# ScalarE's cast of the next pair ahead of VectorE's work on the present one, and four pairs in sevens in blocks 1 to 9 of a decoder layer's gate-and-up products

## The chip, the cores and the metric

The kernel runs on one core of a Trainium2 chip. Its engines are TensorE (PE in the profile: matmuls; PEld: its weight loads), VectorE (DVE), ScalarE (ACT), GpSimd (POOL) and SyncE (SP, which here issues the DMA transfers). The metric is the device time of one execution in microseconds; less is better.

## The reference

The reference is one decoder layer on 256 tokens of width 2048, in float32: a half-FFN, a pair of token mixers (retention and sliding-window attention), a second half-FFN, and a gated embedding, with a layer norm after each. What the change touches most are the two half-FFNs (width 5632):

```
def swiglu(x, w_gu, w_down):
    g, u = jnp.split(x @ w_gu, 2, axis=-1)
    return (jax.nn.silu(g) * u) @ w_down
...
h = layer_norm(alpha * h + 0.5 * swiglu(h, w_ffn1_gu[i], w_ffn1_down[i]), ln_g[i, 0], ln_b[i, 0])
...
mixed = (jax.nn.sigmoid(gate_r) * ret_branch + jax.nn.sigmoid(gate_a) * att_branch) @ w_mix_out[i]
...
h = layer_norm(alpha * h + 0.5 * swiglu(h, w_ffn2_gu[i], w_ffn2_down[i]), ln_g[i, 2], ln_b[i, 2])
ple = jax.nn.sigmoid(h @ w_ple_gate[i]) * (p[i] @ w_ple_proj[i])
```

## The kernel before

**Products in two parts.** Each float32 operand is split into a high part in the format fp32r (`hi`, a cast by ScalarE) and the rest (`lo`, the operand minus `hi`, a subtraction by VectorE). A product is then three matmuls, lo by hi, hi by hi and hi by lo (`Sum.add`, L341 to L343).

**Blocks, pairs and sevens.** A product with a large weight is made in blocks of 1024 columns. A block is a list of units; a unit is a pair of tiles along the inner dimension, and a block over the width of 2048 has eight. A unit of class `Unit` (a plain pair, kind "P") loads one weight tile `raw` of 128x2048, has ScalarE cast it to `hi` (L101) and VectorE subtract `lo` (L102), and takes TensorE 8 products, or 24 matmuls. A unit of class `Seven` (kind "S") makes the same 2 by 2 block product from 7 products, 21 matmuls, in Strassen's way; for that the weights must first be added up:

| step | engine and line | tile |
|---|---|---|
| cast of three quarters of the raw tile | ScalarE, L191 | hb |
| sums u (2 quarters, then 1 and 1) | VectorE, L192, L196, L197 | u |
| casts of the sums (twice 1024) | ScalarE, L193, L198 | hu |
| subtraction lb | VectorE, L202 | lb |
| subtraction lu | VectorE, L205 | lu |

These names carry a prefix of the weight: `lf_gu` in the profile is lo of a plain pair of `f1_gu` or `f2_gu`, `luf_gu` is lu of a seven. The first plain pairs of a block come first and the last pair is plain, so that the end of the sevens (`fold`, `seven_common`, L416) lies inside the block: ScalarE copies a first sum out of PSUM into a tile `eve` (L420), and VectorE makes three operations on it (L423 to L425), which free two of the four PSUM tiles of two banks each. The next block starts in these. VectorE then adds the two other PSUM tiles (L743, twice), ScalarE applies SiLU (L745), and VectorE multiplies gate and up (L748). The result is transposed by TensorE after the second unit of the next block (`turned`, L699, tiles f1t and f2t), and ScalarE copies the transposes out (L700).

**Gate and up.** `w_gu` of each half-FFN is 11 blocks, j = 0 to 10, in the order of `gu_units`. Block 0 is plain. The other odd blocks have four sevens, the even ones three.

**A planner writes the order.** All instructions are in an order fixed by the program. The units of the whole kernel stand in one list, `plan`; `load` issues their DMA on SyncE's queue, up to three units ahead; `step` makes the next unit, a few VectorE instructions at a time; and `pump` takes steps until an estimated VectorE time reaches an estimated TensorE time (`clock`). All of these tiles come from one pool of 23 slots (`SLOTS`). `room` counts what is used of a limit that `weights(n)` sets for each stage: a unit takes 1 slot for its load, 2 (plain) or 5 (seven) while it is made, and keeps 2 or 4 until its matmuls are done. In the gate-and-up blocks the limit falls from 17 to 11 as the activations fill the pool:

```
weights(SLOTS - 5 - (j + 1) // 2 - (2 if j == KF // 4 - 1 else 0))
```

Each engine works through its queue in order. An instruction that waits, for a transfer, another engine or a free slot, holds up all that stands behind it on the same engine.

**The mixers' last product and the norms.** `MIXERS` names the sevens of the mixers' blocks; `w_mix` has two blocks. The last three units of the second (`HELD`) are multiplied first for one half of the tokens, then for the other, so that the norm of the first half runs beside the second. `EVENTS` places the parts of each norm between these units and the first units of the next product: "s" scales a group of columns for one half of the tokens, "t" turns it (transposes, ScalarE's cast, VectorE's subtraction into `ht`). The third entry is the norm ahead of the embedding (`w_pg`).

Of the kernel before, what the change touches and what calls it, by code (L numbers as in the profile page):

```python
# [9 lines left out]
F32R = mybir.dt.float32r  # L10
I32 = mybir.dt.int32
AF = mybir.ActivationFunctionType
ALU = mybir.AluOpType
PSUM = bass.MemoryType.PSUM

P = 128
# [10 lines left out]
KF = FF // P  # L27
# [7 lines left out]
MATMUL = 0.227  # L35
# [18 lines left out]
    ("w_ret", 0): ("PPSPSPSP", (0, 1, 2)),  # L54
    ("w_ret", 1): ("PPSPSPSP", (0, 1, 2)),
    ("w_mix", 0): ("PPPPSPSP", (4, 5)),
    ("w_mix", 1): ("PSPSPPPP", (4, 5)),
}

BIG = 3.0e38  # L60
# [12 lines left out]
        "a6": "c0 m0 s00", "b6": "t00 c1 m1 s10", "c5": "t10", "c6": "s01", "d1": "s11", "d4": "t01", "d5": "t11",  # L73
    },
    {
        "a6": "c0 m0 s00 s01", "b4": "t00", "b6": "t01 c1 m1 s10 s11", "c4": "s02", "c6": "t10", "c7": "t11",
        "d1": "s12", "d4": "t02", "d7": "t12",
    },
)
# [3 lines left out]
def layer(ctx: ExitStack, tc: tile.TileContext, io):  # L83
    nc = tc.nc
    sync, act, dve, pe = nc.sync, nc.scalar, nc.vector, nc.tensor
# [3 lines left out]
    slots = ctx.enter_context(tc.tile_pool(name="slots", bufs=SLOTS))  # L89
# [7 lines left out]
    def slot(shape, dt, name):  # L97
        return slots.tile(shape, dt, tag="slot", name=name)

    def split(dst_hi, dst_lo, src):  # L100
        act.copy(dst_hi, src)  # L101
        dve.tensor_tensor(dst_lo, src, dst_hi, ALU.subtract)  # L102


    plan = []
    GROUP_AT = {"rg": 8, "gr": 21, "ga": 29}

    def halves_of(key):

        name, b, p = key  # L110
        if name.endswith("_gu"):
            return [io[name][2 * b : 2 * b + 2, 1 - c, p // 2, :, p % 2 * 2 : p % 2 * 2 + 2, :] for c in range(2)], True
        if name in GROUP_AT or name in ("w_ret", "w_att"):
            w, at = (io["w_in_f"], GROUP_AT[name]) if name in GROUP_AT else (io[name], 0)
            at += 4 * b
            return [w[at + 2 * c : at + 2 * c + 2, p // 2, :, p % 2 * 2 : p % 2 * 2 + 2, :] for c in range(2)], True
        return [io[name][2 * b + c, p] for c in range(2)], False

    class Unit:


        loads, makes, keeps, steps = 1, 2, 2, 1

        def __init__(self, *key):
            self.key, self.name = key, "_".join(map(str, key))
# [4 lines left out]
        def load(self):  # L130
            self.tile()
            halves, self.grouped = halves_of(self.key)
            for c, src in enumerate(halves):
                self.fetch(2 * c, 2, src.rearrange("g p k n -> p g (k n)") if self.grouped else src)
# [1 line left out]
        def fetch(self, at, n, src, queue=None):  # L136
            (queue or sync).dma_start(self.raw[:, at : at + n], src)

        def make_hi(self):
            self.hi, self.lo = (slot([P, 4, 512], F32R, w + self.name) for w in "hl")  # L140

        def make(self):
            self.make_hi()
            split(self.hi, self.lo, self.raw)
            spend(2048)
            yield

# [22 lines left out]
    class Seven(Unit):  # L170
# [4 lines left out]
        def load(self):  # L175
            self.tile()
            halves, grouped = halves_of(self.key)
            for c, src in enumerate(halves):
# [4 lines left out]
                else:  # L183
                    self.fetch(2 * c, 2, src)

        def make(self):
            raw, nm = self.raw, self.name
            u = slot([P, 4, 512], F32, "u" + nm)
            hb = slot([P, 3, 512], F32R, "hb" + nm)
            hu = slot([P, 4, 512], F32R, "hu" + nm)  # L190
            act.copy(hb, raw[:, 1:])  # L191
            dve.tensor_tensor(u[:, 0:2], raw[:, 1:3], raw[:, 0:1].broadcast_to([P, 2, 512]), ALU.add)  # L192
            act.copy(hu[:, 0:2], u[:, 0:2])  # L193
            spend(1024)
            yield
            dve.tensor_tensor(u[:, 2], raw[:, 2], u[:, 0], ALU.add)  # L196
            dve.tensor_tensor(u[:, 3], u[:, 2], raw[:, 3], ALU.add)  # L197
            act.copy(hu[:, 2:], u[:, 2:])  # L198
            spend(512, 512)
            yield  # L200
            lb, lu = slot([P, 3, 512], F32R, "lb" + nm), slot([P, 4, 512], F32R, "lu" + nm)
            dve.tensor_tensor(lb, raw[:, 1:], hb, ALU.subtract)  # L202
            spend(1536)
            yield
            dve.tensor_tensor(lu, u, hu, ALU.subtract)  # L205
            spend(2048)
            self.b22, self.b11, self.b21 = ((hb[:, j], lb[:, j]) for j in range(3))
            self.t3, self.t1, self.t2, self.t4 = ((hu[:, j], lu[:, j]) for j in range(4))
            yield
# [3 lines left out]
    clock = {"pe": 0.0, "dve": 0.0}  # L213
    loaded, making, ready = [], [], []
    room = {"slots": 0, "used": 0, "far": 3}

    def spend(*sizes):
        for n in sizes:
            clock["dve"] += (n + 150) / 960

    def load():
        while plan and len(loaded) < room["far"]:
            first = loaded[0] if loaded else plan[0]
            if plan[0].loads + first.makes > room["slots"] - room["used"]:
                return
            u = plan.pop(0)
            u.load()
            room["used"] += u.loads
            loaded.append(u)

    def step():

        if not making:
            if not loaded or loaded[0].makes > room["slots"] - room["used"]:
                return False
            u = loaded.pop(0)
            room["used"] += u.makes
            making.append((u, u.make()))
        u, steps = making[0]
        next(steps)  # L240
        u.steps -= 1
        if not u.steps:
            making.pop()
            room["used"] += u.keeps - u.loads - u.makes
            u.made = clock["dve"]
            ready.append(u)
            load()
        return True

    def pump(t):  # L250
        load()
        while clock["dve"] < t and step():
            pass
# [4 lines left out]
    def after(t=None):  # L258

        t = clock["pe"] if t is None else t  # L260
        pump(t)
        clock["dve"] = max(clock["dve"], t)
# [154 lines left out]
    def seven_common(p1, p6, p7, q5):  # L417

        e = slot([P, 4, 512], F32, "eve")
        act.copy(e[:, 1], p1)  # L420
        after()
        spend(512, 512, 1024)
        dve.tensor_tensor(e[:, 0], e[:, 1], p6, ALU.add)  # L423
        dve.tensor_tensor(e[:, 3], e[:, 0], p7, ALU.add)
        dve.tensor_tensor(e[:, 0::2], q5[:, None, :].broadcast_to([P, 2, 512]), e[:, 0::3], ALU.subtract)  # L425
        return e
# [225 lines left out]
    def plain(n):  # L652
        return [("P", p) for p in range(n)]

    def in_order(order, sevens):
        rest = [p for p in range(PAIRS) if p not in sevens]
        sevens = list(sevens)
        return [(kind, (sevens if kind == "S" else rest).pop(0)) for kind in order]

    def gu_units(j):  # L660
        if j == 0:
            return plain(PAIRS)
        order = "PPSSPSSP" if j % 2 else "PPSPSPSP"
        return in_order(order, SEVEN[: order.count("S")])

    def down_units():
# [16 lines left out]
    def ffn(name, i, ht, norm, keep, residual, keepers, away):  # L683
# [26 lines left out]
        for j in range(KF // 4):  # L710
# [12 lines left out]
            def before(u, j=j, offset=offset):  # L723
# [10 lines left out]
                if j == KF // 4 - 1 and u in (4, 6):  # L734
                    convert(u // 2 - 2)

            block(name + "_gu", j, units, rhs, forms, sums, lambda *a: got.append(seven_common(*a)), before)
            if got:
                v = got[0]
# [30 lines left out]
        def fold(b):  # L770
            def f(*a):
                e = seven_common(*a)
                x = y[b].rearrange("p t (c n) -> p (t c) n", c=2)
                spend(2048)
                dve.scalar_tensor_tensor(x, x, 2.0 * ALPHA, e, ALU.mult, ALU.add)
            return f
# [531 lines left out]
    def load_x_chunk(c):  # L1308
        if c % 2 == 0:
            x_parts[c // 2] = slot([P, 8, S], F32, f"xraw{c}")  # L1310
        raw = x_parts[c // 2][:, c % 2 * 4 : c % 2 * 4 + 4]
        pieces = 4 if c == 0 else 1
        parts = [slice(j * 4 // pieces, (j + 1) * 4 // pieces) for j in range(pieces)]
        for at in parts:
            sync.dma_start(raw[:, at], io["xT"][c][:, at])
        if c == 0:
            u = plan.pop(0)
            u.tile()
            u.make_hi()
            halves, u.grouped = halves_of(u.key)  # L1320
            places = []
            for h in range(2):
                for e in range(2):
                    at = u.raw[:, 2 * h + e], u.hi[:, 2 * h + e], u.lo[:, 2 * h + e]
                    act.dma_start(u.raw[:, 2 * h + e], halves[h][e].rearrange("p k n -> p (k n)"))
                    places.append(at)
            room["used"] += u.keeps
            u.made = 0.0
            ready.append(u)
        for j, at in enumerate(parts):  # L1330
            to = ht[:, 4 * c : 4 * c + 4, :][:, at]
            split(to[:, :, :S], to[:, :, S:], raw[:, at])
            spend(1024 // pieces)
            if c == 0:
                split(places[j][1], places[j][2], places[j][0])
# [119 lines left out]
```

## Time and profile before

| | |
|---|---|
| median of three runs | 2288.19 us (2287.73 to 2288.45) |
| the profiled execution | 2287.03 us |
| its span, first to last instruction | 2285.2 us |
| mean granted TensorE clock | 0.998 |
| TensorE busy | 2257.9 us, 99% |
| VectorE busy | 1947.1 us, 85% |
| ScalarE busy | 1184.9 us, 52% |

Busy time is the time in which an engine executes; matmuls are pipelined, so that TensorE's is modelled at their ends. In a timeline, a line gives the start in us from the span's beginning, the duration, engine, source line and operation, the tile written and the tile read, and in brackets how long the engine sat idle before it and for whom. In the groups, the idle time and its causes stand behind the last bar. The times come from one profiled execution.

### The profile page before, as it was taken

How to read it: one execution, taken by the hardware profiler on the slowest of the kernel's cores; microseconds unless marked ns; L12 is line 12 of the kernel's file. 1: busy time of each engine (PE TensorE's matmuls, PEld its weight loads, DVE VectorE, ACT ScalarE, POOL GpSimd, SP SyncE). 2: the span in 40 equal slices, each digit the busy share in tenths (PEclk: the TensorE clock that was granted, in tenths of full speed). 3: DMA queues.
4: the chain of work that ended last, by engine and by line, in shares of the span. 5: the costliest groups of instructions: out<-in, count | busy, mean ns of one | idle time of the engine just before them, and what ended most of it. 6: DMA issues, size and time to landing. Idle time of an engine off the chain costs nothing.

```text
span 2285.2 us, 26799 instructions
## 1 busy us (share of the span) xinstructions
PE 2257.9 (99%) x10418; PEld 1871.4 (82%) x10418; DVE 1947.1 (85%) x1704; ACT 1184.9 (52%) x988; POOL 0.7 (0%) x6
## 2 busy tenths in 40 slices
PE   8999999999999999999999999999999999999997
PEld 7888888888888888888887778888888888888876
DVE  6999898888897879678898667989989889889876
ACT  5555554555454435454545565455555556555541
POOL 0000000000000000000000000000000000000000
PEclk9999999999999999999999999999999999999999
DMA  9666565655677546445657454676656557465861
GB/s 319 205 197 190 186 206 189 196 194 190 239 278 258 203 147 217 143 170 166 217 184 230 145 196 169 256 256 204 201 185 221 184 173 233 149 233 207 312 240 56
DMA packets 236399, 465.33 MB, mean 204 GB/s; under 512 B 17136, under 2 KB 105968, under 8 KB 233712
## 3 DMA queue, kind: packets, MB, share of 16 engines
q1 hardware_dynamic: 234256, 459.87, 59.3%
q10 hardware_dynamic: 2016, 3.76, 0.5%
q8 instruction: 82, 1.34, 0.2%
q14 instruction: 45, 0.37, 0.0%
HBM read 455.17 MB, written 8.39 MB: 203 GB/s over the span
## 4 chain that ended last, share of the span: by engine, by line
PE 92%; DVE 5%; ACT 1%; DMA 1%; issue 1%; SPq 0%; DVEq 0%; ACTq 0%
PE f1g L343 5%; PE f1g L341 5%; PE f1g L342 5%; PE f2g L341 4%; PE f2g L342 4%; PE f2g L343 4%; PE rqk L305 3%; PE f1d L343 1%; PE f2d L341 1%; PE f1d L342 1%; PE f2d L343 1%; PE f2d L342 1%; PE f1d L341 1%; PE f1e L343 1%; PE f1e L342 1%; PE f1e L341 1%
## 5 line engine op out<-in xcount | busy, mean ns | idle before, releaser
L102 DVE TENSOR_TENSOR lf_gu<-rf_gu,hf_gu 128x2048 fp32r<-128x2048 f32 (+1 forms) x109 | 239.7, 2227 | 42.9 <-ACT hf_gu L101 42.9
L101 ACT CAST hf_gu<-rf_gu 128x2048 fp32r<-128x2048 f32 (+1 forms) x109 | 199.9, 1862 | 31.4 <-DMA rf_gu<-in_f_gu 19.6
L341 PE MATMUL f1g<-hf_gu,xt 128*128 128x512 f32 x424 | 166.4, 392 | 6.2 <-ACT hf_gu L101 5.9
L343 PE MATMUL f1g<-lf_gu,xt 128*128 128x512 f32 x424 | 166.1, 392 | 1.6 <-DVE lf_gu L102 1.6
L342 PE MATMUL f1g<-hf_gu,xt 128*128 128x512 f32 x424 | 165.9, 391 | 0.0
L205 DVE TENSOR_TENSOR luf_gu<-uf_gu,huf_gu 128x2048 fp32r<-128x2048 f32 x70 | 159.9, 2285 | 1.5
L102 DVE TENSOR_TENSOR lf_down<-rf_down,hf_down 128x2048 fp32r<-128x2048 f32 x60 | 136.6, 2288 | 20.7 <-ACT hf_down L101 16.9
L193 ACT CAST huf_gu<-uf_gu 128x1024 fp32r<-128x1024 f32 x70 | 73.7, 1053 | 131.4 <-DVE uf_gu L192 105.9
L341 PE MATMUL f2g<-hf_gu,ht 128*128 128x512 f32 x360 | 140.1, 389 | 0.4 <-DVE eve L425 0.4
L343 PE MATMUL f2g<-lf_gu,ht 128*128 128x512 f32 x360 | 140.1, 389 | 0.0
L342 PE MATMUL f2g<-hf_gu,ht 128*128 128x512 f32 x360 | 140.1, 389 | 0.0
L202 DVE TENSOR_TENSOR lbf_gu<-rf_gu,hbf_gu 128x1536 fp32r<-128x1536 f32 x70 | 122.6, 1751 | 12.3 <-ACT hbf_gu L191 12.3
L101 ACT CAST hf_down<-rf_down 128x2048 fp32r<-128x2048 f32 x60 | 114.3, 1913 | 35.6 <-DMA rf_down<-in_f_down 8.1
L191 ACT CAST hbf_gu<-rf_gu 128x1536 fp32r<-128x1536 f32 x70 | 103.6, 1479 | 20.9 <-DMA rf_gu<-in_f_gu 15.7
L341 PEld LDWEIGHTS f1g<-hf_gu,xt 128*128 128x128 f32 x424 | 80.2, 189 | 23.7 <-ACT hf_gu L101 6.3
L343 PEld LDWEIGHTS f1g<-lf_gu,xt 128*128 128x128 f32 x424 | 80.1, 189 | 18.8 <-DVE lf_gu L102 2.3
L342 PEld LDWEIGHTS f1g<-hf_gu,xt 128*128 128x128 f32 x424 | 80.3, 189 | 16.7
L192 DVE TENSOR_TENSOR uf_gu<-rf_gu 128x1024 f32<-128x1024 f32 x70 | 85.3, 1219 | 4.0 <-DMA rf_gu<-in_f_gu 1.7
L198 ACT CAST huf_gu<-uf_gu 128x1024 fp32r<-128x1024 f32 x70 | 73.7, 1053 | 26.3 <-DVE uf_gu L197 26.2
L745 ACT ACTIVATE eve<-eve 128x1024 f32<-128x1024 f32 x20 | 21.2, 1062 | 117.7 <-DVE eve L743 117.7
L341 PEld LDWEIGHTS f2g<-hf_gu,ht 128*128 128x128 f32 x360 | 67.6, 188 | 14.9 <-issue 0.8
L343 PEld LDWEIGHTS f2g<-lf_gu,ht 128*128 128x128 f32 x360 | 67.6, 188 | 14.0
(1241 smaller groups left out, 6238.6 us busy)
## 6 DMA issues: line engine op xcount, KB each, us to landing
rf_gu<-in_f_gu SPq DMA_DIRECT2D x210, 512.0 KB, 5.8
rf_down<-in_f_down SPq DMA_DIRECT2D x176, 512.0 KB, 4.5
rf_gu<-in_f_gu SPq DMA_DIRECT2D x280, 256.0 KB, 4.4
rw_rv<-in_w_rv SPq DMA_DIRECT2D x32, 512.0 KB, 4.8
rga<-in_w_in_f SPq DMA_DIRECT2D x32, 512.0 KB, 5.5
rw_mix<-in_w_mix SPq DMA_DIRECT2D x32, 512.0 KB, 4.4
rw_pg<-in_w_pg SPq DMA_DIRECT2D x32, 512.0 KB, 5.2
rrg<-in_w_in_f SPq DMA_DIRECT2D x24, 512.0 KB, 4.9
```

Source lines behind the costliest of these rows:

```text
L101: act.copy(dst_hi, src)
L102: dve.tensor_tensor(dst_lo, src, dst_hi, ALU.subtract)
L191: act.copy(hb, raw[:, 1:])
L192: dve.tensor_tensor(u[:, 0:2], raw[:, 1:3], raw[:, 0:1].broadcast_to([P, 2, 512]), ALU.add)
L193: act.copy(hu[:, 0:2], u[:, 0:2])
L198: act.copy(hu[:, 2:], u[:, 2:])
L202: dve.tensor_tensor(lb, raw[:, 1:], hb, ALU.subtract)
L205: dve.tensor_tensor(lu, u, hu, ALU.subtract)
L305: pe.matmul(ps[:, f], u.tile_of(kk)[0][:, f * P : (f + 1) * P], rhs(k), start=k == 0, stop=k == KD - 1,)
L341: pe.matmul(o, al, bh, start=first, stop=False)
L342: pe.matmul(o, ah, bh, start=False, stop=False)
L343: pe.matmul(o, ah, bl, start=False, stop=self.left == 0)
```

## The change

It has five parts. (1) The cast of a unit becomes a method of its own, `high`. The planner calls it for the next loaded unit at each step of the present one, where a slot is free, and counts that slot. (2) In gate and up, blocks 1 to 9 have four sevens and only block 10 has three. (3) The second `w_mix` block has one seven in place of two. (4) In the norm before the embedding, scaling the third group of the first half of the tokens comes four places later ("c8" for "c4"). (5) `seven_common` lets the planner go ahead up to 15 matmuls before the end of the last seven, before ScalarE's copy into `eve` is written down.

```diff
-    ("w_mix", 1): ("PSPSPPPP", (4, 5)),
+    ("w_mix", 1): ("PSPPPPPP", (4,)),
...
-        "a6": "c0 m0 s00 s01", "b4": "t00", "b6": "t01 c1 m1 s10 s11", "c4": "s02", "c6": "t10", "c7": "t11",
+        "a6": "c0 m0 s00 s01", "b4": "t00", "b6": "t01 c1 m1 s10 s11", "c6": "t10", "c7": "t11", "c8": "s02",
...
         loads, makes, keeps, steps = 1, 2, 2, 1
+        cast = False
...
-        def make_hi(self):
-            self.hi, self.lo = (slot([P, 4, 512], F32R, w + self.name) for w in "hl")
+        def high(self):
+            self.hi = slot([P, 4, 512], F32R, "h" + self.name)
+            act.copy(self.hi, self.raw)
 
         def make(self):
-            self.make_hi()
-            split(self.hi, self.lo, self.raw)
+            self.lo = slot([P, 4, 512], F32R, "l" + self.name)
+            dve.tensor_tensor(self.lo, self.raw, self.hi, ALU.subtract)
...
+        def high(self):
+            self.hb = slot([P, 3, 512], F32R, "hb" + self.name)
+            act.copy(self.hb, self.raw[:, 1:])
+
         def make(self):
-            raw, nm = self.raw, self.name
+            raw, hb, nm = self.raw, self.hb, self.name
             u = slot([P, 4, 512], F32, "u" + nm)
-            hb = slot([P, 3, 512], F32R, "hb" + nm)
             hu = slot([P, 4, 512], F32R, "hu" + nm)
-            act.copy(hb, raw[:, 1:])
...
-            if plan[0].loads + first.makes > room["slots"] - room["used"]:
+            if plan[0].loads + first.makes - first.cast > room["slots"] - room["used"]:
                 return
...
+    def cast(u):
+        if not u.cast:
+            u.high()
+            u.cast = True
+            room["used"] += 1
+
     def step():
 
         if not making:
-            if not loaded or loaded[0].makes > room["slots"] - room["used"]:
+            if not loaded or loaded[0].makes - loaded[0].cast > room["slots"] - room["used"]:
                 return False
+            cast(loaded[0])
             u = loaded.pop(0)
-            room["used"] += u.makes
+            room["used"] += u.makes - 1
             making.append((u, u.make()))
+        if loaded and room["slots"] > room["used"]:
+            cast(loaded[0])
         u, steps = making[0]
...
         e = slot([P, 4, 512], F32, "eve")
+        pump(clock["pe"] - 15 * MATMUL)
         act.copy(e[:, 1], p1)
...
-        order = "PPSSPSSP" if j % 2 else "PPSPSPSP"
+        order = "PPSSPSSP" if j < KF // 4 - 1 else "PPSPSPSP"
```

More of the change, by code (lines that the diff above doesn't have):

```diff
@@ L1318, in load_x_chunk @@
             u.tile()
-            u.make_hi()
+            u.hi, u.lo = (slot([P, 4, 512], F32R, w + u.name) for w in "hl")
             halves, u.grouped = halves_of(u.key)
```

## The prediction

> **What bounds the kernel now.** I read the page's busy table and chain, then stretches of one block each, then VectorE's and ScalarE's timelines, then the groups with their waits.
>
> ```profile
> span 2285.2 us, 26799 instructions
> PE 2257.9 (99%) x10418; PEld 1871.4 (82%) x10418; DVE 1947.1 (85%) x1704; ACT 1184.9 (52%) x988; POOL 0.7 (0%) x6
> PE 92%; DVE 5%; ACT 1%; DMA 1%; issue 1%; SPq 0%; DVEq 0%; ACTq 0%
> ```
>
> TensorE is busy all the time and carries 92% of the chain: time goes only if matmuls go, or the few holes in it close. The profiled execution took 2287.03 us, 1.8 us beyond its span, 1.16 us below the median of the three runs (2288.19). Their spread is under 0.8 us, yet I take 0.2% (4.6 us) as the least difference that a measurement tells from none.
>
> A gate-and-up block is 8 pairs; a plain pair costs TensorE 24 matmuls, a pair in sevens 21. The stretches below run from one block's transposes (f1t, f2t) to the next: blocks 7, 8 and 9 of the first half-FFN, 8 and 9 of the second.
>
> ```profile
> core 0: us, PE busy (x) PEld busy (x) DVE busy (x) ACT busy (x) POOL busy (x), PEclk, DMA share, GB/s
> 318.32:360.01 41.69, 41.69 (x190) 34.61 (x189) 38.09 (x30) 23.74 (x19) 0.00 (x0) 1.00 0.54 173
> 360.01:402.39 42.38, 42.38 (x193) 35.18 (x192) 36.30 (x26) 20.57 (x16) 0.00 (x0) 1.00 0.63 199
> 402.39:444.75 42.36, 41.98 (x189) 34.49 (x189) 37.56 (x28) 22.16 (x17) 0.00 (x0) 1.00 0.61 198
> 1831.92:1874.29 42.37, 42.37 (x193) 35.17 (x192) 36.56 (x26) 20.57 (x16) 0.00 (x0) 1.00 0.63 199
> 1874.29:1916.66 42.37, 41.98 (x190) 34.50 (x189) 37.57 (x28) 22.15 (x17) 0.00 (x0) 1.00 0.62 199
> ```
>
> Block 7 (four sevens) takes 41.69 us without a hole, block 8 (three) 42.38. The 0.68 us (42.37 - 41.69) are three matmuls of 0.227 us. Block 9 also has four sevens but takes 42.36: it loses 0.67 us, in both half-FFNs. TensorE sets the pace; the question is whether VectorE can feed it.
>
> ```profile
> 324.93 1.22 DVE L192 TENSOR_TENSOR uf_gu<-rf_gu 128x1024 f32<-128x1024 f32 x1
> 326.19 0.69 DVE L196 TENSOR_TENSOR uf_gu<-rf_gu,uf_gu 128x512 f32<-128x512 f32 x1
> 326.91 0.69 DVE L197 TENSOR_TENSOR uf_gu<-uf_gu,rf_gu 128x512 f32<-128x512 f32 x1
> 327.52 1.75 DVE L202 TENSOR_TENSOR lbf_gu<-rf_gu,hbf_gu 128x1536 fp32r<-128x1536 f32 x1
> 329.19 2.28 DVE L205 TENSOR_TENSOR luf_gu<-uf_gu,huf_gu 128x2048 fp32r<-128x2048 f32 x1
> 331.39 4.48 DVE L102 TENSOR_TENSOR lf_gu<-rf_gu,hf_gu 128x2048 fp32r<-128x2048 f32 x2
> ...
> 345.90 0.68 DVE L423 TENSOR_TENSOR eve<-eve,f_gu7s 128x512 f32<-128x512 f32 x1
> ...
> 348.48 2.28 DVE L102 TENSOR_TENSOR lf_gu<-rf_gu,hf_gu 128x2048 fp32r<-128x2048 f32 x1
> ...
> 435.53 2.35 DVE L743 TENSOR_TENSOR eve<-eve,f1g 128x1024 f32<-128x1024 f32 x2
> 437.80 2.28 DVE L205 TENSOR_TENSOR luf_gu<-uf_gu,huf_gu 128x2048 fp32r<-128x2048 f32 x1
> 440.00 1.22 DVE L748 TENSOR_TENSOR eve<-eve 128x1024 f32<-128x1024 f32 x1
> 441.13 2.28 DVE L102 TENSOR_TENSOR lf_gu<-rf_gu,hf_gu 128x2048 fp32r<-128x2048 f32 x1
> ```
>
> From start to start, a seven takes VectorE 331.39 - 324.93 = 6.46 us and a plain pair 4.48 - 2.28 = 2.20. The end of a block costs 2.58 (three eve operations, 345.90 to 348.48), 2.27 (two L743, 435.53 to 437.80) and 1.13 (L748). Four sevens: 4 x 6.46 + 4 x 2.20 + 5.98 = 40.6 us in 41.69, room for 1.07 us of idling. Three sevens: 36.4 in 42.37. Blocks alternate now, so VectorE may idle 7 us in two blocks, and does:
>
> ```profile
> L102 DVE TENSOR_TENSOR lf_gu<-rf_gu,hf_gu 128x2048 fp32r<-128x2048 f32 x105 | 237.0, 2285 | 40.5 <-ACT hf_gu L101 40.5
> L101 ACT CAST hf_gu<-rf_gu 128x2048 fp32r<-128x2048 f32 x105 | 197.5, 1910 | 29.1 <-DMA rf_gu<-in_f_gu 17.4 <-PE f2g L342 4.3 <-PE f1g L342 3.4
> ...
> L202 DVE TENSOR_TENSOR lbf_gu<-rf_gu,hbf_gu 128x1536 fp32r<-128x1536 f32 x70 | 122.6, 1751 | 12.3 <-ACT hbf_gu L191 12.3
> ...
> L191 ACT CAST hbf_gu<-rf_gu 128x1536 fp32r<-128x1536 f32 x70 | 103.6, 1479 | 20.9 <-DMA rf_gu<-in_f_gu 15.7 <-PE f2g L342 1.6 <-PE f1g L342 1.4
> ```
>
> ```profile
> DVE eve L748 <- ACT eve L745: 11.9, 10, 1.2
> ...
> DVE eve L423 <- ACT eve L420: 7.2, 6, 1.6
> ```
>
> In the 22 gate-and-up blocks it idles 40.5 + 12.3 us, 2.4 per block, for ScalarE's casts. One case shows how:
>
> ```profile
> 402.43 1.02 ACT L700 COPY f1a<-f1t 128x1024 f32<-128x1024 f32 x1 [4.45 <-PE f1t L699]
> 403.34 1.91 ACT L101 CAST hf_gu<-rf_gu 128x2048 fp32r<-128x2048 f32 x1
> ```
>
> ```profile
> 405.28 2.29 DVE L102 TENSOR_TENSOR lf_gu<-rf_gu,hf_gu 128x2048 fp32r<-128x2048 f32 x1 [4.52 <-ACT hf_gu L101]
> ...
> 431.28 0.69 DVE L423 TENSOR_TENSOR eve<-eve,f_gu9s 128x512 f32<-128x512 f32 x1 [1.60 <-ACT eve L420]
> ```
>
> The cast that VectorE needs stands in ScalarE's queue behind a copy (L700) that waits 4.45 us for transposes. VectorE idles 4.52 us in block 9, is late from then on, and reaches the eve operations only at 431.28; they free the banks that block 10 starts in.
>
> **The change part by part.**
>
> *Matmuls.* Blocks 2, 4, 6 and 8 of both half-FFNs get a fourth seven: 8 x 0.68 = 5.44 us off TensorE's path, if VectorE keeps up. Each also gives VectorE 6.46 - 2.20 = 4.26 us more. The second w_mix block loses a seven: +0.68 us. Together 21 matmuls fewer.
>
> *Cast ahead.* It adds no work and reorders ScalarE's queue. In the changed program's order of instructions, the casts of the next pair stand in front of the f1t copy (in block 9 those of the third plain pair and of the second seven's sums; only the plain one stood behind it), and the next seven's cast stands in front of the present seven's sum casts. The copy then no longer delays what VectorE needs at once. I expect most of the 2.4 us per block to go. Bounds: none of it goes, 2.4 us stay, 1.3 over the room; all goes, and VectorE is ahead.
>
> I check VectorE against TensorE's due times in a steady block, time 0 at TensorE's start, with the L743 pair there, the eve operations already done and one operation (1.26 us) of the first seven. TensorE needs 5.45 us per plain pair and 4.77 per seven, and 0.87 for the transposes:
>
> ```profile
> 359.14 0.87 PE f1t L699 x8
> ```
>
> VectorE finishes the first seven at 2.27 + 5.20 + 1.13 = 8.6 (due 11.8), the second at 15.1 (16.5), the plain pair at 17.3 (21.3), the sevens at 23.7 (26.7) and 30.2 (31.5), three plain pairs at 36.8, and the eve operations at 39.4 (banks due 41.7). The least slack is 1.3 us, and each wait of VectorE of over that in one block costs TensorE the excess.
>
> *What may wait now.* A cast put ahead waits for its load, and behind it stand the present seven's sum casts, for which VectorE's last subtraction waits, and the eve copy.
>
> ```profile
> rf_gu<-in_f_gu SPq DMA_DIRECT2D x280, 256.0 KB, 4.4
> ```
>
> ```profile
> 75.46 1.90 SPq L182 DMA_DIRECT2D rf_gu<-in_f_gu  x4
> ```
>
> Four issues take 1.9 us and the last lands about 4.4 later, so I count 6.5 us. By the order of instructions, the fourth seven's load starts when TensorE has finished the block's first pair (5.5): landed at 12, its cast wanted at 17 to 18. The next block's first seven is loaded after the third plain pair (26.7): landed at 33.2, cast by 34.8, the eve copy behind it by 35.4, wanted at 36.8. Both are in time, the second by 1.4 us. I count the new wait at nothing; bounds: nothing, or all the load waits in the rows above (17.4 + 15.7 us, 1.5 per block).
>
> *Where holes close.* In the first line of the following, w_mix's held pairs wait for a lo that VectorE makes late; with a seven less it comes 4.3 us earlier, TensorE 0.68 later. The next is the turn before the embedding. The last, with the delay around it, is block 9's 0.67, there in both half-FFNs.
>
> ```profile
> PE mo L343 <- DVE lw_mix L102: 0.8, 1, 0.8
> PE w_pg L341 <- DVE ht L102: 0.6, 1, 0.6
> ...
> PE f1g L341 <- DVE eve L425: 0.4, 1, 0.4
> ```
>
> ```profile
> 2189.37 1.28 DVE L476 SCALAR_TENSOR_TENSOR f2y<-f2y,mv,ln_g 128x1024 f32<-128x1024 f32 x1
> 2190.69 1.28 DVE L477 SCALAR_TENSOR_TENSOR f2y<-f2y,rstd,ln_b 128x1024 f32<-128x1024 f32 x1
> 2191.89 1.28 DVE L102 TENSOR_TENSOR ht<-lnps,ht 128x512 fp32r<-128x512 f32 x2
> ```
>
> Before the embedding, VectorE scales a third group (1.28 + 1.28 us) ahead of the two ht subtractions on which TensorE waits; the change puts it behind them, worth the whole 0.6 us wait.
>
> Sum: -5.44 + 0.68 - 0.8 (w_mix) - 1.34 (block 9, twice) - 0.6 = -7.5 us. The span goes to 2277.7, its execution to 2279.5, the median to 2280.7 us (-0.33%).
>
> **The rivals.**
>
> *The holes stay, or others as large come.* Only the 21 matmuls go: 21 x 0.227 = 4.8 us, 2283.4. For it: block 10 has the fewest buffers, and the end of a block has only 1 to 3 us of slack. Against it: each hole's cause is moved in the order of instructions. Chance 0.14.
>
> *VectorE's operations do not overlap at the higher load.* With each at its whole duration, a seven is 1.22 + 0.69 + 0.69 + 1.75 + 2.28 = 6.63 us, a plain pair 2.28, the end of a block 6.2: 41.9 us. Eighteen blocks at 0.2 over TensorE give back 3.7 us: 2284.4, no change. Against it: 2.20 from start to start in the rows above. Chance 0.08. [...]
>
> *Slower: casts ahead block ScalarE on loads.* The idling changes its cause and stays: 1.5 us per block for loads, and for the SiLU and the eve copy (11.9 + 7.2) / 22 = 0.87, so 2.4 against 1.07 of room. Eighteen blocks at 1.3 over give +23.4 us: 2304. It decides for slower once VectorE's idling, with no load early enough to catch up, passes 1.07 + 7.5 / 18 = 1.49 us per block. For it: two blocks that shared 7 us of idle room now share 2.1. Against: the due times above. Chance 0.12.
>
> *The change does not do what it says*: the casts stay where they were for want of a buffer. The order of instructions shows them moved in all of blocks 2 to 9, so I give it nothing.
>
> **How the numbers follow.** The forecast has 0.66: 2280.7 us, its own range 2279.3 (if the 1.16 us between the profiled execution and the median go the other way) to 2282.5 (the w_mix hole and one of 1 us stay). Range: 2279.3 to 2286: it takes in the first two rivals, the second with the w_mix and embedding holes still open (2284.4 + 1.4), and leaves out the slower one. Faster by over 0.2% means below 2283.6: the forecast and half of the first rival, 0.73. Within 0.2%: the other half, the second rival and a little of the third, 0.17. Slower 0.10.
>
> **What would show it.** Right: blocks 1 to 9 at 41.69 us each in both half-FFNs, VectorE's idling before lf_gu and lbf_gu from 52.8 us to under 20, no wait of TensorE for eve in them, none of 0.8 for lw_mix. Wrong: blocks of 42 us or more with TensorE waiting for luf_gu, lbf_gu or eve, and ScalarE waiting for loads ahead of huf_gu; or VectorE starting its subtractions 2.28 us apart.

## The result and the profile after

The changed kernel takes 2281.03 us (median of 7 runs, 2279.72 to 2283.58); the kernel before, run beside it, 2288.45 us (2287.73 to 2290.11). The ratio is 0.9968, with a 95% interval of 0.9956 to 0.998: 7.4 us, 0.32% faster. The forecast was 2280.7 us in 2279.3 to 2286.

The head of the page of the changed kernel:

```profile
span 2281.8 us, 26816 instructions
PE 2253.8 (99%) x10397; PEld 1867.9 (82%) x10397; DVE 1973.0 (86%) x1732; ACT 1196.8 (52%) x1002; POOL 0.7 (0%) x6
```

TensorE has the 21 matmuls fewer (10418 - 10397) and VectorE 26 us more work. Blocks 8 and 9 of the first half-FFN and block 9 of the second, in the columns that the prediction used:

```profile
358.94:400.64 41.70, 41.70 (x191) 34.62 (x189) 40.41 (x31) 23.98 (x20) 0.00 (x0) 1.00 0.62 202
400.64:442.33 41.69, 41.69 (x190) 34.61 (x189) 40.42 (x29) 22.35 (x18) 0.00 (x0) 1.00 0.62 202
1871.28:1912.97 41.69, 41.69 (x190) 34.61 (x189) 39.66 (x29) 22.34 (x18) 0.00 (x0) 1.00 0.61 202
```

All blocks 1 to 9 of both half-FFNs take 41.69 or 41.70 us, with TensorE busy throughout. The groups of VectorE and ScalarE in gate and up, with what ended their idling (the lines have moved: L142 is the cast of a plain pair, L190 that of a seven, L146, L206 and L209 the subtractions):

```profile
L146 DVE TENSOR_TENSOR lf_gu<-rf_gu,hf_gu 128x2048 fp32r<-128x2048 f32 x97 | 218.3, 2284 | 8.6 <-ACT hf_gu L142 8.6
L209 DVE TENSOR_TENSOR luf_gu<-uf_gu,huf_gu 128x2048 fp32r<-128x2048 f32 x78 | 178.2, 2284 | 6.0 <-ACT huf_gu L202 5.9
L190 ACT CAST hbf_gu<-rf_gu 128x1536 fp32r<-128x1536 f32 x78 | 114.3, 1483 | 86.0 <-DMA rf_gu<-in_f_gu 58.5
L206 DVE TENSOR_TENSOR lbf_gu<-rf_gu,hbf_gu 128x1536 fp32r<-128x1536 f32 x78 | 136.6, 1751 | 0.0
```

Before lf_gu and lbf_gu VectorE idled 52.8 us, now 8.6. ScalarE in turn waits 58.5 us for loads in front of a seven's cast, where it waited 15.7. VectorE's own idling now stands mostly in front of the eve operations, in its list of waits:

```profile
DVE eve L437 <- ACT eve L434: 21.0, 17, 1.8
```

In gate and up the copy L434 itself idles for no matmul. In blocks 1 to 4 it stands behind the casts of the sums, and VectorE idles 1.6 to 1.85 us for these, 13.4 us in all. In blocks 5 to 9 it stands right behind the cast that was put ahead, that of the next block's first seven, which waits 3.7 to 5.4 us, in eight of ten cases for its load; VectorE idles up to 1.7 us for it, 7.6 us in all. ScalarE and VectorE in block 9 of the first half-FFN:

```profile
424.38 1.48 ACT L190 CAST hbf_gu<-rf_gu 128x1536 fp32r<-128x1536 f32 x1 [4.35 <-DMA rf_gu<-in_f_gu]
425.76 0.58 ACT L434 COPY eve<-f_gu9s 128x512 f32<-128x512 f32 x1
```

```profile
426.37 0.69 DVE L437 TENSOR_TENSOR eve<-eve,f_gu9s 128x512 f32<-128x512 f32 x1 [0.85 <-ACT eve L434]
```

So the chain of the prediction's slower rival is there, but VectorE has the room for it and TensorE does not wait in these blocks. TensorE's own waits:

```profile
PE f1g L354 <- ACT hf_gu L101: 7.1, 1, 7.1
PE f1g L356 <- DVE lf_gu L146: 1.6, 1, 1.6
...
PE f_down0s L356 <- DVE lbf_down L206: 0.6, 1, 0.6
...
PE w_ret L354 <- DVE eve L439: 0.4, 1, 0.4
```

The waits for lw_mix (0.8), ht (0.6) and, at block 10, eve (0.4 in each half-FFN) are gone. New are one for lbf_down in the first down stage and one before w_ret.

**The profiled execution tells less than the median.** It took 2283.58 us, the longest of the seven, so against the profiled execution of before the gain is 3.45 us, not 7.4. Where it goes is seen by putting the same instruction of both traces side by side: the transposes at the end of block 0, after block 9, a product of the mixers, the transposes of the norm ahead of the second half-FFN, those after its block 9, and those before the embedding. TensorE's timeline of before:

```profile
65.09 1.03 PE L699 MATMUL f1t<-ident,f1v 128*128 128x128 f32 x8
443.72 1.03 PE L699 MATMUL f1t<-ident,eve 128*128 128x128 f32 x8
1191.90 0.50 PE L1056 MATMUL as<-trig,aq 64*128 64x128 f32 x4
1473.04 1.03 PE L509 MATMUL lnps<-ident,mixy 128*128 128x128 f32 x8
1915.63 1.03 PE L699 MATMUL f2t<-ident,eve 128*128 128x128 f32 x8
2198.20 1.03 PE L509 MATMUL lnps<-ident,f2y 128*128 128x128 f32 x8
```

and of after:

```profile
66.93 1.03 PE L713 MATMUL f1t<-ident,f1v 128*128 128x128 f32 x8
442.17 1.03 PE L713 MATMUL f1t<-ident,eve 128*128 128x128 f32 x8
1192.54 0.50 PE L1070 MATMUL as<-trig,aq 64*128 64x128 f32 x4
1473.61 1.03 PE L523 MATMUL lnps<-ident,mixy 128*128 128x128 f32 x8
1912.81 1.03 PE L713 MATMUL f2t<-ident,eve 128*128 128x128 f32 x8
2194.56 1.04 PE L523 MATMUL lnps<-ident,f2y 128*128 128x128 f32 x8
```

| stretch | after less before, us | forecast, us |
|---|---|---|
| start and block 0 | +1.84 | 0 |
| blocks 1 to 9, first half-FFN | -3.39 | 4 x -0.68 - 0.67 = -3.39 |
| block 10, down, mixers up to the attention | +2.19 | 0 |
| rest of the mixers, w_mix | -0.07 | +0.68 - 0.8 = -0.12 |
| second half-FFN, blocks 1 to 9 | -3.39 | -3.39 |
| its block 10, down, turn before the embedding | -0.82 | -0.6 |
| the rest | +0.24 | 0 |
| sum (the span) | -3.40 | -7.5 |

Where the change acts, the terms are met to 0.25 us. The 4 us beside them are a late start and waits in the first down stage and before w_ret. With each matmul of one trace beside the same of the other, the changed kernel falls back by 1.1 us at the wait for lbf_down and by 1.1 us more at those before w_ret, though TensorE idles only 0.6 us at each.

**The start** is a matter of the clock. TensorE waits 1.59 us for the first lf_gu in both traces, but after it the two go apart. Stretches of 3.41 us of the changed kernel, with the granted clock in the third column from the right:

```profile
13.65:17.06 3.41, 1.77 (x7) 0.84 (x6) 2.29 (x1) 2.55 (x3) 0.00 (x0) 1.00 1.03 395
17.06:20.47 3.41, 3.41 (x10) 2.67 (x9) 3.40 (x2) 2.28 (x2) 0.00 (x0) 0.50 0.94 323
```

and of the kernel before:

```profile
14.77:18.18 3.41, 1.82 (x9) 1.44 (x9) 3.03 (x2) 2.85 (x2) 0.00 (x0) 1.00 1.00 364
18.18:21.59 3.41, 3.41 (x17) 2.83 (x16) 2.84 (x3) 1.92 (x1) 0.00 (x0) 1.00 1.04 365
```

After a stretch with 1.77 us of matmuls the clock is at half for 3.41 us (10 matmuls instead of 17); after one with 1.82 us it is not. What decides between the two was not shown. Where the stretches begin was read from the clock's changes in the traces: in the changed kernel the half clock lasts 3.413 us from 17.06 us on, and the next fall, at 2269.86 us, comes 660 such lengths after the first; in the kernel before the clock falls at 2274.4 us, 661 such lengths after 18.18. In these two traces the stretches lie differently over the same wait: it begins 1.42 us into the one of the changed kernel and 0.08 us into that of the kernel before. Of both kernels some runs have a mean clock of 0.997, some of 0.998. Of the runs with a clock on record, those at 0.997 have a median of 2289.0 us before and 2281.5 after, those at 0.998 2287.9 and 2280.5: the gain is 7.4 to 7.5 us in both. So I take the start for no part of the change.

### The profile page after: what moved, and what is told of

It reads as the page before. It is cut to its first block, busy times and chain, and to the rows that moved or that the text cites. A ratio compares the mean times of both kernels' runs of the same rounds, so it can differ in the third digit from the quotient of the medians.

```text
span 2281.8 us, 26816 instructions
## 1 busy us (share of the span) xinstructions
PE 2253.8 (99%) x10397; PEld 1867.9 (82%) x10397; DVE 1973.0 (86%) x1732; ACT 1196.8 (52%) x1002; POOL 0.7 (0%) x6
## 4 chain that ended last, share of the span: by engine, by line
PE 92%; DVE 5%; DMA 2%; ACT 1%; issue 1%; SPq 0%; DVEq 0%; ACTq 0%
PE f1g L356 5%; PE f1g L355 5%; PE f1g L354 5%; PE f2g L355 4%; PE f2g L356 4%; PE f2g L354 4%; PE rqk L318 3%; PE f2d L356 1%; PE f2d L354 1%; PE f2d L355 1%; PE f1e L355 1%; PE f1e L354 1%; PE f1e L356 1%; PE f1d L355 1%; PE f1d L354 1%; PE rqk L326 1%
## 5 line engine op out<-in xcount | busy, mean ns | idle before, releaser
L146 DVE TENSOR_TENSOR lf_gu<-rf_gu,hf_gu 128x2048 fp32r<-128x2048 f32 x97 | 218.3, 2284 | 8.6 <-ACT hf_gu L142 8.6
L142 ACT CAST hf_gu<-rf_gu 128x2048 fp32r<-128x2048 f32 x97 | 183.7, 1909 | 23.7 <-DMA rf_gu<-in_f_gu 16.0
L209 DVE TENSOR_TENSOR luf_gu<-uf_gu,huf_gu 128x2048 fp32r<-128x2048 f32 x78 | 178.2, 2284 | 6.0 <-ACT huf_gu L202 5.9
L354 PE MATMUL f1g<-hf_gu,xt 128*128 128x512 f32 x392 | 154.1, 393 | 7.2 <-ACT hf_gu L101 7.1
L190 ACT CAST hbf_gu<-rf_gu 128x1536 fp32r<-128x1536 f32 x78 | 114.3, 1483 | 86.0 <-DMA rf_gu<-in_f_gu 58.5
L356 PE MATMUL f1g<-lf_gu,xt 128*128 128x512 f32 x392 | 153.7, 392 | 1.6 <-DVE lf_gu L146 1.6
L355 PE MATMUL f1g<-hf_gu,xt 128*128 128x512 f32 x392 | 153.7, 392 | 0.0
L146 DVE TENSOR_TENSOR lf_down<-rf_down,hf_down 128x2048 fp32r<-128x2048 f32 x60 | 136.4, 2286 | 12.9 <-ACT hf_down L142 11.5
L197 ACT CAST huf_gu<-uf_gu 128x1024 fp32r<-128x1024 f32 x78 | 82.0, 1052 | 116.3 <-DVE uf_gu L196 113.6
L142 ACT CAST hf_down<-rf_down 128x2048 fp32r<-128x2048 f32 x60 | 114.2, 1913 | 46.9 <-DMA rf_down<-in_f_down 20.3
L206 DVE TENSOR_TENSOR lbf_gu<-rf_gu,hbf_gu 128x1536 fp32r<-128x1536 f32 x78 | 136.6, 1751 | 0.0
L356 PE MATMUL f2g<-lf_gu,ht 128*128 128x512 f32 x328 | 127.6, 389 | 0.0
L354 PE MATMUL f2g<-hf_gu,ht 128*128 128x512 f32 x328 | 127.6, 389 | 0.0
L355 PE MATMUL f2g<-hf_gu,ht 128*128 128x512 f32 x328 | 127.6, 389 | 0.0
L202 ACT CAST huf_gu<-uf_gu 128x1024 fp32r<-128x1024 f32 x78 | 82.1, 1053 | 27.9 <-DVE uf_gu L201 27.7
L354 PEld LDWEIGHTS f2g<-hf_gu,ht 128*128 128x128 f32 x328 | 61.6, 188 | 12.8
L355 PEld LDWEIGHTS f2g<-hf_gu,ht 128*128 128x128 f32 x328 | 61.6, 188 | 12.8
```

Of the source, the lines that this page charges most:

```text
L142: act.copy(self.hi, self.raw)
L146: dve.tensor_tensor(self.lo, self.raw, self.hi, ALU.subtract)
L190: act.copy(self.hb, self.raw[:, 1:])
L354: pe.matmul(o, al, bh, start=first, stop=False)
L355: pe.matmul(o, ah, bh, start=False, stop=False)
L356: pe.matmul(o, ah, bl, start=False, stop=self.left == 0)
```

## The experiments

All were run beside the kernel before, whose medians lie between 2288.66 and 2288.87 us.

**The order of the sevens alone.** The kernel before, with

```
-        order = "PPSSPSSP" if j % 2 else "PPSPSPSP"
+        order = "PPSSPSSP" if j < KF // 4 - 1 else "PPSPSPSP"
```

> The kernel before with one part of the change: four sevens also in blocks 2, 4, 6 and 8; the casts stay where they were, w_mix and the turn before the embedding too. Theory (VectorE has room for 1.07 us of idling per block, and idles 2.4 us for ScalarE as long as the casts stand behind what waits): blocks 2 to 9 settle near 43.0 us with TensorE waiting for los or eve, 18 x 1.3 - 5.4 = +18 us, 2306 us, slower than before. Rival (the casts' place does not matter, VectorE's sum alone does, 40.6 us): blocks at 41.69 us and 2288.4 - 5.4 = 2283 us.

Measured: 2284.46 us (11 runs, 2283.09 to 2285.23), ratio 0.9981 (0.9972 to 0.999): 4.2 us faster. The theory fell by 22 us. Block 3, in the same columns:

```profile
150.21:192.63 42.42, 41.96 (x189) 34.50 (x188) 36.49 (x28) 22.68 (x18) 0.00 (x0) 1.00 0.57 187
```

Only block 3 loses anything of note, 0.73 us, in both half-FFNs alike; the others run at 41.69 to 41.72 us with the casts where they were. VectorE's idling for these casts fell by itself:

```profile
L102 DVE TENSOR_TENSOR lf_gu<-rf_gu,hf_gu 128x2048 fp32r<-128x2048 f32 (+1 forms) x101 | 221.2, 2222 | 25.4 <-ACT hf_gu L101 25.2
L202 DVE TENSOR_TENSOR lbf_gu<-rf_gu,hbf_gu 128x1536 fp32r<-128x1536 f32 x78 | 136.6, 1751 | 6.0 <-ACT hbf_gu L191 6.0
```

Of the 25.2 us, 22.2 stand before tiles of 128x2048. With the 6.0 that is 28.2 us, against 52.8 in the kernel before; in blocks 4 to 9 it is 0 to 0.6 us per block. VectorE's timeline, at the los of block 3 and of block 8, tells why:

```profile
154.13 2.29 DVE L102 TENSOR_TENSOR lf_gu<-rf_gu,hf_gu 128x2048 fp32r<-128x2048 f32 x1 [4.23 <-ACT hf_gu L101]
...
363.35 2.29 DVE L102 TENSOR_TENSOR lf_gu<-rf_gu,hf_gu 128x2048 fp32r<-128x2048 f32 x1 [0.60 <-ACT hf_gu L101]
```

and ScalarE's, at the same two places:

```profile
151.28 1.01 ACT L700 COPY f1a<-f1t 128x1024 f32<-128x1024 f32 x1 [4.55 <-PE f1t L699]
152.19 1.91 ACT L101 CAST hf_gu<-rf_gu 128x2048 fp32r<-128x2048 f32 x1
...
360.50 1.02 ACT L700 COPY f1a<-f1t 128x1024 f32<-128x1024 f32 x1 [0.53 <-PE f1t L699]
361.41 1.91 ACT L101 CAST hf_gu<-rf_gu 128x2048 fp32r<-128x2048 f32 x1
```

The cast stands behind the copy in both. But the copy is ready at a time that TensorE sets; a VectorE that is early waits 4.23 us for what comes behind it, one that has more to do arrives later and waits 0.60. The idling was the slack itself, not a cost on top of it, except in block 3, where it was more than the room.

**The casts ahead alone.** The changed kernel with the three orders of before:

```
-    ("w_mix", 1): ("PSPPPPPP", (4,)),
+    ("w_mix", 1): ("PSPSPPPP", (4, 5)),
-        ... "c6": "t10", "c7": "t11", "c8": "s02",
+        ... "c4": "s02", "c6": "t10", "c7": "t11",
-        order = "PPSSPSSP" if j < KF // 4 - 1 else "PPSPSPSP"
+        order = "PPSSPSSP" if j % 2 else "PPSPSPSP"
```

> The changed kernel with the orders of before (three sevens in blocks 2, 4, 6, 8; two in the second w_mix block; the scaling ahead of the ht subtractions): only the casts are ahead. Theory: the hole of 0.67 us in block 9 closes in both half-FFNs and nothing else of size moves: 2288.4 - 1.3 = 2287.1 us; VectorE's idling before lf_gu and lbf_gu falls from 52.8 us as in the changed kernel and turns into idling for the eve copy. Rival (block 9's hole comes from the banks or the transposes themselves): it stays, 2288.4 us.

Measured: 2288.91 us (11 runs, 2287.47 to 2291.32), ratio 1.0002 (0.9993 to 1.0011): no gain. Block 9 of both half-FFNs:

```profile
401.20:443.06 41.86, 41.86 (x189) 34.53 (x188) 36.98 (x28) 21.69 (x17) 0.00 (x0) 1.00 0.69 225
1873.69:1915.66 41.97, 41.95 (x190) 34.53 (x188) 36.95 (x28) 21.63 (x17) 0.00 (x0) 1.00 0.70 227
```

```profile
PE mo L356 <- DVE lw_mix L146: 0.7, 1, 0.7
PE w_pg L354 <- DVE ht L102: 0.6, 1, 0.6
...
PE rg L354 <- DVE eve L439: 0.3, 1, 0.3
```

The hole in block 9 shrinks from 0.67 to 0.17 and 0.28, as the theory has it, but its 0.9 us are not seen in the time: by the trace they are given back in the mixers, the wait for rg (0.3) among it. The waits for lw_mix and ht are those of before, so it is the orders of w_mix and of the turn that close them, not the casts. VectorE's idling does not turn into idling for the eve copy, as was expected: 25.3 us of it now stand before luf_gu, for the casts of the sums, 15.3 before lf_gu and 8.9 before eve.

**One and three additions more for VectorE.** The changed kernel, with n = 1 and n = 3 in

```
             dve.tensor_tensor(u[:, 2], raw[:, 2], u[:, 0], ALU.add)
+            if self.key[0].endswith("_gu") and self.key[1] < KF // 4 - 1 and self.key[2] == 0:
+                for _ in range(n):
+                    dve.tensor_tensor(u[:, 2], raw[:, 2], u[:, 0], ALU.add)
```

> The changed kernel with one addition of 128x512 done twice in the first seven of blocks 1 to 9 of gate and up (0.72 us from start to start, the same result): VectorE's load rises to 41.3 us in blocks of 41.69. Theory (room of 1.07 us per block): blocks stay at 41.69 us and the time within 1 us of the changed kernel's 2281.0; only the idling before eve shrinks. Rival (VectorE's operations do not overlap, 41.9 us per block, no room): + 18 x 0.72 = +13 us, 2294 us.

> The same with three such additions more: 2.16 us, VectorE's load 42.8 us per block. Theory (room 1.07 us): blocks 2 to 9 at 42.8 us, + 18 x 1.09 = +19.6 us, 2300.6 us. If the room is as large as the longest idling before eve in the changed kernel (1.85 us): + 5.6 us, 2286.6. If there is none: +39 us, 2320.

Measured: 2281.65 us (6 runs) with one and 2300.51 us (5 runs, 2299.89 to 2301.79) with three; expected were 2281.0 and 2300.6. With one, the idling before eve shrinks from 21.0 to 12.5 us and blocks stay at 41.69 us. With three, a late block of the first half-FFN is

```profile
409.17:451.89 42.72, 41.98 (x189) 34.53 (x188) 42.34 (x32) 23.85 (x19) 0.00 (x0) 1.00 0.66 212
```

VectorE waits for nothing in blocks 8 and 9, so 42.72 - 2.16 = 40.56 us is its load of a block with four sevens; the prediction summed it to 40.6 from starts, and to 41.9 from whole durations. The time of 2300.51 us agrees better than its parts: 42.8 us was expected of all blocks from 2 on, but only blocks 6 to 9 come to 42.7 to 42.9 us, while blocks 1 to 5 lie between 41.69 and 44.32. The 18 blocks together lose 20.6 us for 19.6 expected.

**The three orders without the casts ahead.** The kernel before with the edits to gu_units, MIXERS and EVENTS alone.

> The changed kernel without its casts ahead: the kernel before with all three orders changed (four sevens in blocks 1 to 9, one seven less in w_mix, the scaling behind the ht subtractions). New theory (VectorE's idling for casts is slack that goes by itself when VectorE is full; the casts ahead are worth the one hole of 0.73 us in block 3 of each half-FFN, and cost 0.6 to 0.9 in the down stage): within 1 us of the changed kernel, 2281 to 2282.5. Rival (the casts ahead are worth nearly the whole difference of 3.4 us that the first experiment left, w_mix and the embedding 0.7 of it): 2283.8 us.

Measured: 2283.76 us (11 runs, 2281.53 to 2284.68), ratio 0.9977 (0.9968 to 0.9986); the changed kernel again, beside it, 2281.43. So the orders of w_mix and of the turn are worth 0.7 us in the medians (2284.46 - 2283.76; the prediction's terms make 0.72), which is no more than the runs tell apart: the two intervals overlap. The casts ahead are worth 2.3 to 2.7 us, as the rival had it, and the traces agree: from the transposes of block 0 to the end it is 2217.2 us here and 2214.9 in both traces of the changed kernel. Of this the hole of block 3, twice, is 1.5; the traces show 0.5 more in waits of the mixers for gr and w_ret. The cost in the down stage that the theory gave to the casts is there without them:

```profile
PE f_down0s L343 <- DVE lbf_down L202: 0.6, 1, 0.6
```

**The changed kernel again.**

> The changed kernel once more, beside the others on one chip: 2281.0 us within 1. If the waits for lbf_down (0.6 us) and before w_ret (0.4 + 0.2) belong to the program, its trace has them again; if they belong to the one execution, it does not.

Measured: 2281.43 us (7 runs, 2280.11 to 2283.38). Its trace has the wait for lbf_down (0.6) and that before w_ret (0.4) again, so they are no accident of one execution. But the order of the instructions alone does not make the wait for lbf_down: up to w_mix the kernel with the order of the sevens alone has the same order as that with the three orders, and its trace is without this wait.

**The residual's load later.** The changed kernel with

```
-            if u == 11:
+            if u == 13:
                 y[0] = load_columns(residual, 0, name + "y")
```

> The changed kernel with the load of the residual's first half in down (1 MB) issued two pairs later, behind the load of the seven whose lo TensorE waits for. Theory (that load arrives late since the residual's load stands ahead of it, 533.2 against 538.4 us): the 0.6 us wait for lbf_down goes, and 0.9 us of the time. Rival (it is the two further weight loads, 2 to 3.6 us earlier than before, that share the transfer with it): the wait stays, no change.

Measured: 2281.03 us (7 runs, 2280.02 to 2282.42). The wait for lbf_down is gone from the trace, as the theory has it. Why it arises stays open, for it is not how near the loads stand: from the residual's load to the next weight load it is 5.2 us in the changed kernel, which waits, and 5.2 in that with the casts alone, which does not; 7.1 us with the three orders, which waits, and 7.1 with the order of the sevens alone, which does not. The span is 1.0 us shorter than that of the changed kernel's second profile (2280.6 against 2281.6), the median 0.4 us, which is less than the runs tell apart.

**Four sevens in block 10.** The changed kernel with

```
-        order = "PPSSPSSP" if j < KF // 4 - 1 else "PPSPSPSP"
+        order = "PPSSPSSP"
```

> The changed kernel with four sevens in block 10 too. TensorE has 3 matmuls less in each half-FFN (-1.36 us together). VectorE is busy for 39.6 us of block 10's 42.4 in the changed kernel, since it also makes the first los of down and f1ac; 4.26 us more are 43.9 in 41.7. Theory (VectorE becomes the bound): no gain, block 10 or the first down block 1 to 2 us longer, 2281 to 2284 us. Rival (what VectorE makes there ahead for down can wait): 2279.7 us.

Measured: 2287.74 us (11 runs, 2284.52 to 2291.70): the gain is lost. Block 10 of the first half-FFN, and VectorE's and TensorE's waits in it:

```profile
439.97:483.44 43.47, 41.99 (x189) 34.53 (x188) 39.12 (x28) 26.51 (x21) 0.00 (x0) 1.00 0.61 216
```

```profile
461.01 2.29 DVE L209 TENSOR_TENSOR luf_gu<-uf_gu,huf_gu 128x2048 fp32r<-128x2048 f32 x1 [0.81 <-ACT huf_gu L202]
```

```profile
PE f_gu10s L356 <- DVE luf_gu L209: 3.0, 2, 1.5
```

The block grows by 1.1 us instead of shrinking by 0.7, as the theory has it, but not by VectorE's sum: that is busy for 39.1 of 43.5 us. It is late at one seven, before which it waits three times for ScalarE: 0.60 us for a plain pair's cast, 2.06 for that of f1ac (the activations for down), and the 0.81 above. What slows the median by more than the trace shows was not settled.

**Three additions, casts where they were.** The kernel of the three orders alone, with n = 3 as above.

> The three extra additions of the first seven (2.16 us per block, VectorE the bound), but in the kernel with the three orders changed and the casts where they were. Theory (a cast behind the transposes' copy stops VectorE only while VectorE is early; late, it finds the cast done): blocks 5 to 9 at 42.7 us as with the casts ahead, time 2300.5 + 2.4 = 2303 us. Rival (each block loses the 0.6 us that VectorE idled before lf_gu in blocks 6 to 9 with the orders alone): 43.3 us per block, 2303 + 18 x 0.6 = 2314 us.

Measured: 2304.47 us (5 runs, 2303.0 to 2306.6). Blocks 6 to 9 take 42.75 to 42.91 us against 42.71 to 42.87 with the casts ahead, not 43.3. Where VectorE is the bound it finds the casts done in either place; there the theory holds. Block 5 is at 43.4 us in both kernels, where 42.7 was expected.

**Two loads ahead, with and without the casts ahead.** In both kernels

```
-    room = {"slots": 0, "used": 0, "far": 3}
+    room = {"slots": 0, "used": 0, "far": 2}
```

> The changed kernel with at most two weight loads ahead instead of three, so that a cast ahead has to wait longer for its load. The prediction's slower rival (a cast that waits for its load holds up the sum casts and the eve copy behind it): ScalarE's wait for loads before hbf_gu rises well over 58.5 us, blocks go to 42.5 us or more with TensorE waiting for luf_gu or eve, 2295 us or more. Theory (due times leave 1.4 us and ScalarE is free for 18 us of a block): blocks stay at 41.7 us, 2281 to 2284 us.

> The same with the casts where they were (three orders changed): if late loads hurt through ScalarE's queue, this one loses less than the one with casts ahead does against its own three loads (2281 and 2283.8 us); if they hurt through TensorE's or VectorE's wait for the data itself, both lose the same.

Measured: 2308.34 us (4 runs, 2304.20 to 2311.41) with the casts ahead, 27 us more than with three loads; 2296.30 us (7 runs, 2294.24 to 2296.50) with the casts where they were, 12.5 more. Here the prediction's slower rival has its price. ScalarE, VectorE and TensorE at the end of block 3 of the second half-FFN, casts ahead:

```profile
1650.26 1.49 ACT L190 CAST hbf_gu<-rf_gu 128x1536 fp32r<-128x1536 f32 x1 [3.47 <-DMA rf_gu<-in_f_gu]
1653.35 1.48 ACT L190 CAST hbf_gu<-rf_gu 128x1536 fp32r<-128x1536 f32 x1 [1.60 <-DMA rf_gu<-in_f_gu]
...
1656.63 0.58 ACT L434 COPY eve<-f_gu3s 128x512 f32<-128x512 f32 x1
```

```profile
1657.23 0.69 DVE L437 TENSOR_TENSOR eve<-eve,f_gu3s 128x512 f32<-128x512 f32 x1 [2.10 <-ACT eve L434]
```

```profile
1660.05 0.47 PE L354 MATMUL f2g<-hf_gu,ht 128*128 128x512 f32 x1 [0.41 <-DVE eve L439]
```

Two casts wait 3.47 and 1.60 us for loads, the eve copy stands behind them, VectorE idles 2.10 us for it, and TensorE waits for the banks. The 18 blocks lose 9.9 us over 41.69 each in this kernel; in the other 2.0, of which 1.5 are block 3's hole from before. More than half of the loss lies outside these blocks, where it was not followed; one part of it in this profile is a single wait of 8.2 us before the embedding that the profile puts down to nothing.

**Four loads ahead.** The changed kernel with "far" at 4.

> The changed kernel with up to four weight loads ahead instead of three. Theory (with three, no cast ahead is late enough to reach TensorE in gate and up): blocks 1 to 9 stay at 41.69 us; outside them, the 0.6 us wait for lbf_down and the 0.4 to 0.6 before w_ret may close, 2280 to 2281 us. Rival (more loads in flight share the transfers with the one that is needed first, and take buffers): new waits for los, 2283 us or more.

Measured: 2291.14 us (11 runs, 2289.83 to 2293.12). Blocks 1 to 9 stay at 41.69 us, the wait of ScalarE for loads before hbf_gu falls from 58.5 to 5.0 us and the wait for lbf_down in the first down stage goes; but elsewhere sevens are made late:

```profile
PE w_mix1s L356 <- DVE lbw_mix L206: 3.0, 1, 3.0
PE f_down1s L356 <- DVE lbf_down L206: 1.9, 2, 1.1
```

The rival was right as to the waits and the time; which of its two reasons holds, shared transfers or buffers, was not tried. ScalarE's 58.5 us of waiting cost TensorE nothing in gate and up of the changed kernel: without them its blocks are not faster.

## Why the prediction was right, and where its reasons were not

- **The time.** 2281.03 us was measured for 2280.7, faster by 0.32% for 0.33%. The two profiled spans differ by 3.4 us only, since the profiled execution of before lies 1.4 us under its median and that of after 2.55 over. Of these 4 us, 1.84 are the clock and the start; the other 2.2 are the delays at lbf_down and before w_ret, which the forecast did not have. Whether they are there in runs without a profile stays open; if they are, something unseen makes up for them, and that the median meets the forecast to 0.3 us is luck. The lower end of the forecast's own range does not follow from its reason: 1.16 us the other way gives 2278.3 us, not 2279.3. The result does not touch it.
- **The matmuls.** -5.44 us for eight more sevens: blocks of 41.69 in place of 42.37, to the hundredth. The w_mix stretch gave -0.07 for -0.12, the turn before the embedding -0.82 for -0.6, and the two orders together 0.7 us in the medians for 0.72, there within the noise.
- **VectorE's load and room.** 40.6 us summed, 40.56 measured from the three additions; room for one addition and not for three, with the times of both within 0.7 us of what was expected: a rival room of 1.85 us or of none is out. The rival of operations that do not overlap falls with it: it would have made the block with three additions 44 us long, and the steady ones were 42.72.
- **Cast ahead: the step that failed.** The prediction took the 2.4 us per block that VectorE idled for ScalarE as a cost that has to be removed before the sevens fit, and let the casts ahead remove it. The sevens fit without (2284.46 us, not 2306): the idling fell by itself once VectorE had more to do, from 52.8 to 28.2 us, and to 0.6 or less per block in blocks 4 to 9. What the casts ahead buy is one hole of 0.73 us in each half-FFN and about 1 us elsewhere; without the sevens they buy nothing.
- **Block 9's hole.** -1.34 us came, but either part closes it: the order alone makes block 9 41.69 us long, the casts alone 41.86 and 41.97. The cast behind the copy cost TensorE something only where VectorE idled 4.2 to 4.5 us in one block of four sevens, in block 9 before and in block 3 with the order alone; blocks 5 and 7 before, with 1.9 to 2.7 us, lost nothing. Why VectorE comes so early in just these blocks was not followed: blocks 3, 5 and 7 before stand behind a block of three sevens as block 9 does.
- **What may wait now.** The new wait was counted at nothing, with an upper bound of 1.5 us per block for all of ScalarE's waiting for loads. That waiting rose to 16.0 + 58.5 us, 3.4 per block, over twice the bound. The eve copy, forecast 1.4 us in time, came late for VectorE by 0.8 us per block in blocks 5 to 9; TensorE lost nothing in the 18 blocks, since VectorE had the room. The margin is one load: with two ahead instead of three the same queue costs 9.9 us in these blocks.
- **Holes stay, or others come.** This rival was half right: the old holes closed, but 0.6 us for lbf_down and 0.4 to 0.6 before w_ret came in, outside the blocks that the prediction looked at. The first goes when the residual's load is moved, though why it arises stays open. The second is there with the casts where they were too (0.6 us with the order of the sevens alone, 0.8 with the three orders); its cause was not tried.

## What to carry to other kernels

Idling of an engine that has slack says when it was early, not what it would lose if it had more to do (here 52.8 us of it for casts fell to 28.2 with eight more sevens): sum its work from start to start, compare the sum with the time of the engine that sets the pace, and test the room by adding work of a known size. An instruction that waits for a transfer, put ahead in its queue, cost TensorE nothing here with three loads ahead and 9.9 us with two; take one load away to see how near the edge is. A profile of one execution can differ from the median by more than a small change brings (here by 2.55 us, where the casts ahead are worth 2.3 to 2.7), so put the same instructions of both traces side by side, and read the start apart.

## What the runs showed of the hardware

The half clock came after a hole of 1.59 us in the changed kernel, and not after one of 1.59 us in the kernel before. A stretch of 3.41 us in which TensorE was busy for 1.77 us was followed by 3.41 us at half clock (above), one with 1.82 us was not. In the kernel with four loads ahead this stretch, with two waits in w_mix in and behind it, was followed by 6.82 us at half clock:

```profile
1437.70:1441.11 3.41, 0.98 (x3) 0.49 (x3) 3.41 (x3) 2.82 (x3) 0.00 (x0) 1.00 0.10 7
1441.12:1447.94 6.82, 5.76 (x14) 4.52 (x15) 6.82 (x4) 2.40 (x3) 0.00 (x0) 0.50 0.38 150
```

In its 3.41 us at half clock the changed kernel ran 10 matmuls, the kernel before 17 in the same length at full clock: the hole of 1.59 us cost 7 matmuls of 0.227 us more, about as much again. The clock was lowered here after stretches with matmuls in 0.52 and in 0.29 of them, with a longest wait of 1.59 us in the changed kernel's, and was not after one with matmuls in 0.53 of it.
